# A two-layer decoder trunk on one core: first weight reads held behind a small write, output projections with three seven-product pairs and two added pairs, and new orders of the pieces in every kind of unit

## The chip, the cores and the metric

The kernel runs on one core of one Trainium2 chip; the other cores are idle. The metric is the device time of one execution in microseconds. The kernel before took 2147.89 us (median of three runs, 2144.24 to 2151.99). Lower is better.

## The reference

Two layers over x (256 tokens, 2048 features, float32). Each layer normalises x, projects it with w_in to gated linear attention (GLA) and stick-breaking attention heads, maps the heads' outputs with w_o, adds that to x, and adds a squared-ReLU MLP with 8192 hidden features. Cut to what the change touches:

```python
def hybrid_layer(x, attn_norm, w_in, ..., w_o, mlp_norm, w_up, w_down):
    h = rms_norm(x, attn_norm)
    proj = jnp.einsum('bsd,de->bse', h, w_in)
    ...
    mixed = jnp.concatenate([o_gla, o_sb], axis=-1)
    x = x + jnp.einsum('bse,ed->bsd', mixed, w_o)
    hm = rms_norm(x, mlp_norm)
    up = jnp.square(jax.nn.relu(jnp.einsum('bsd,df->bsf', hm, w_up)))
    return x + jnp.einsum('bsf,fd->bsd', up, w_down)
```

## The kernel before

**One product.** Every float32 weight and operand is split into a high part (rounded to the type float32r) and a low part (what is left). One product of a 128x128 block of the operand with a 128x512 piece of weights is three matmuls into one PSUM bank: high by high, high by low, low by high (L1198 to L1200; L613 to L615 in the older stages). The names in the profile are whi and wlo for a weight's parts: ACT copies raw to whi (L1066, the *cast*), DVE subtracts it from raw to get wlo (L1070, the *subtraction*). Four wlo buffers and five whi buffers (LOWS, RING) let both run ahead of PE.

**Units and steps.** From the first projection on, the work consists of *units* of 256 tokens by 1024 columns, with a depth of 2048 in 8 *pairs* of 128 rows. The kinds are g (the second GLA gate, 8 plain steps), o (output projection, two halves o0 and o1), up and down (MLP, four quarters of 8192, each with two up and two down units), and iv, ik, iq (a projection of the next layer, or of layer 0 at the start). A unit accumulates into eight PSUM banks; each pair's share of two token blocks by two column blocks is computed in one of three ways:
- *slow* pair: 8 products in two steps of four, 24 matmuls. Two casts and two subtractions of 128x1024.
- *fast* (seven-product) pair: the seven products of a Strassen scheme in four steps of 6, 6, 6 and 3 matmuls. DVE forms sums of the weights (L858: ts<-raw of 128x1024, raw<-ts,raw and raw<-raw of 128x512) and four subtractions, three of 128x1024 and one of 128x512. The operand needs sums too (forms, L439: four small DVE operations, L454 to L457, a copy on ACT, L471, and a subtraction on DVE, L475).
- *added* pair: 8 products in two steps of 12 matmuls, without DVE. POOL issues a DMA that reads the weights from HBM and rounds them on the way into a tile chi (L1033). ACT writes its negative into a tile dlo (L1037, the *negation*). POOL issues a second DMA that reads the same weights and adds them to dlo (L1040, the *correction*), which leaves the low part. There are three chi buffers (CAST) and two dlo buffers (ADDS).

**What sets the order.** In a unit, a list of pair numbers sets the order of the steps on PE (EACH, FEWER, MORE, OWN, L24 to L28; the two tuples behind a list name the fast and the added pairs). unit_order (L865) picks the list. A planner (Plan.run, L81) then lays all pieces of a phase out, with assumed lengths and due times, and so fixes the order of instructions on ACT and DVE; PE, SP and POOL keep the order in which the pieces were made. Each engine then runs its queue in that order, and waits in it. There are three phases: one before layer 0's attention (l = -1: iv, ik, iq of layer 0), and one behind the attention of each layer (l = 0: g, o, MLP, then iv, ik, iq of layer 1; l = 1: g, o, MLP).

**The opening.** Before the phase l = -1, SP loads x in four blocks, a vector of norm gains (t, 16 KB) and the first weights. PE turns x with the identity matrix ident, which POOL builds; it also turns the gains to a column (L334, copied by DVE in L335) which ACT needs for each operand cast (L500). 13 transposes of ident (L563) fill PE's time while it waits. Then 96 matmuls of a first value projection follow (L613 to L615) into acc_145; x blocks 1 to 3 are turned in between.

## Time and profile before

| | us |
|---|---|
| median of three runs | 2147.89 |
| the profiled execution | 2145.96 |
| its span, first to last instruction | 2144.3 |
| PE busy | 2124.8 |
| DVE busy | 1944.5 |
| ACT busy | 1403.3 |
| POOL busy | 234.5 |

The granted TensorE clock of the execution was 0.997 on average. PE's instructions are pipelined, so that "busy" says little of how fast it works: it has to be read by the distance of two starts in the timeline. Stages by first matmul, from the span's start: opening 13.9 to 42.2, iv/ik/iq of layer 0 to 163, attention of layer 0 to 299.5, gate unit and output projections to 370, MLP to 1090, iv/ik/iq of layer 1 to 1196, attention to 1359, gate unit and output projections to 1430, MLP to the end.

### The profile page before, as it was taken

To read this page: it belongs to the slowest core of one execution; us is meant where nothing else is said; L and a number is where in the kernel's file an instruction comes from. 1 tells how busy PE (TensorE), PEld (TensorE's weight loads), DVE (VectorE), ACT (ScalarE), POOL (GpSimd) and SP (SyncE) were. 2 spreads that over 40 slices of the span, in tenths; PEclk is the share of its full clock that TensorE was granted. 3 is DMA by queue.
4 is the path that set the end of the run, shared out by engine and by line. 5 is a ranking of instruction groups with operands and counts; after the bars stand their busy time and mean duration, and the time that the engine had idled before them with its cause. 6 is when DMAs were issued, how large, how long until landed. Compare 5 with 4: busy or idle time off the path is not lost.

```text
span 2144.3 us, 28255 instructions
## 1 busy us (share of the span) xinstructions
PE 2124.8 (99%) x10076; PEld 1765.1 (82%) x10076; DVE 1944.5 (91%) x2636; ACT 1403.3 (65%) x1853; POOL 234.5 (11%) x362
## 2 busy tenths in 40 slices
PE   8999999999999999999999999999999999999999
PEld 6788888888888888888888988888888888888887
DVE  5988878999999999999999796699999999999998
ACT  6666666676577566667766575666765765765764
POOL 0110000011111111111111100000111111111110
PEclk9999999999999999999999999999999999999999
DMA  7885365588888988988888644756888888888886
GB/s 247 245 236 179 118 187 196 167 246 252 258 251 246 268 239 253 266 245 238 252 258 251 191 138 137 224 162 204 260 241 258 254 258 247 246 255 256 248 244 196
DMA packets 146992, 488.74 MB, mean 228 GB/s; under 512 B 10298, under 2 KB 19074, under 8 KB 146852
## 3 DMA queue, kind: packets, MB, share of 16 engines
q1 hardware_dynamic: 103076, 327.55, 44.7%
q0 software_dynamic: 43776, 159.40, 31.6%
q8 instruction: 79, 1.29, 0.2%
q14 instruction: 61, 0.50, 0.1%
HBM read 484.81 MB, written 2.10 MB: 227 GB/s over the span
## 4 chain that ended last, share of the span: by engine, by line
PE 55%; issue 36%; POOL 5%; DMA 2%; DVE 1%; ACT 1%; POOLq 0%
POOL dlo L1040 3%; PE acc L613 3%; PE acc L615 2%; PE acc L614 2%; POOL chi L1033 2%; DMA dlo<-in_w_up_dram 1%; DMA dlo<-in_w_in_dram 1%; DMA dlo<-in_w_down_dram 1%; PE ps L1780 0%; DVE wlo L596 0%; DMA chi<-in_w_in_dram 0%; PE ps L724 0%; PE ps L1730 0%; PE ps L1773 0%; PE ps L778 0%
## 5 line engine op out<-in xcount | busy, mean ns | idle before, releaser
L1066 ACT ACTIVATE whi<-raw 128x1024 fp32r<-128x1024 f32 (+1 forms) x701 | 653.2, 955 | 364.6 <-DVE raw L858 209.9
L1070 DVE TENSOR_TENSOR wlo<-raw,whi 128x1024 fp32r<-128x1024 f32 (+1 forms) x701 | 760.9, 1091 | 70.0 <-ACT whi L1066 21.7
L1037 ACT ACTIVATE dlo<-chi 128x1024 fp32r<-128x1024 f32 x152 | 159.9, 1053 | 83.0 <-DMA chi<-in_w_in_dram 13.9
L1066 ACT ACTIVATE whi<-ts 128x1024 fp32r<-128x1024 f32 x165 | 174.4, 1057 | 53.5 <-DVE ts L858 29.2
L858 DVE TENSOR_TENSOR ts<-raw 128x1024 f32<-128x1024 f32 x165 | 200.7, 1216 | 3.9 <-DMA raw<-in_w_down_dram 2.2
L1070 DVE TENSOR_TENSOR wlo<-ts,whi 128x1024 fp32r<-128x1024 f32 x165 | 200.8, 1217 | 0.4 <-PE m__631_2940 L1199 0.2
L613 PE MATMUL acc<-whi,act 128*128 128x512 f32 (+2 forms) x384 | 142.1, 370 | 2.6 <-ACT whi L594 2.6
L615 PE MATMUL acc<-whi,act 128*128 128x512 f32 (+2 forms) x384 | 137.6, 358 | 0.0
L614 PE MATMUL acc<-wlo,act 128*128 128x512 f32 (+2 forms) x384 | 137.4, 358 | 0.0
L594 ACT ACTIVATE whi<-raw 128x1024 fp32r<-128x1024 f32 (+2 forms) x98 | 88.1, 906 | 64.7 <-PE acc L615 64.3
L596 DVE TENSOR_TENSOR wlo<-raw,whi 128x1024 fp32r<-128x1024 f32 (+2 forms) x98 | 100.4, 1030 | 30.4 <-ACT whi L594 29.5
L1033 POOL DMA_DIRECT2D chi<-in_w_up_dram x64 | 35.4, 555 | 759.2 <-PE m__2836_13416 L1200 142.1
L858 DVE TENSOR_TENSOR raw<-raw 128x512 f32<-128x512 f32 x165 | 112.8, 684 | 1.3
L858 DVE TENSOR_TENSOR raw<-ts,raw 128x512 f32<-128x512 f32 x165 | 112.5, 682 | 0.1
L1033 POOL DMA_DIRECT2D chi<-in_w_down_dram x64 | 35.4, 554 | 524.2 <-PE m__3624_17092 L1200 33.1
L1292 ACT ACTIVATE act<-act,st 128x512 f32<-128x512 f32 x88 | 60.5, 715 | 46.5 <-DVE act L858 46.4
L613 PEld LDWEIGHTS acc<-whi,act 128*128 128x128 f32 x384 | 72.9, 190 | 15.3 <-issue 3.4
L615 PEld LDWEIGHTS acc<-whi,act 128*128 128x128 f32 x384 | 72.9, 190 | 10.6
L614 PEld LDWEIGHTS acc<-wlo,act 128*128 128x128 f32 x384 | 73.0, 190 | 9.3 <-DVE wlo L596 0.4
L1040 POOL DMA_DIRECT2D dlo<-in_w_down_dram x64 | 54.7, 854 | 68.4 <-ACT dlo L1037 66.0
L475 DVE TENSOR_TENSOR act<-t,act 128x512 fp32r<-128x512 f32 x90 | 61.1, 682 | 0.0
L1040 POOL DMA_DIRECT2D dlo<-in_w_up_dram x64 | 54.8, 856 | 56.7 <-ACT dlo L1037 55.4
(4156 smaller groups left out, 5738.9 us busy)
## 6 DMA issues: line engine op xcount, KB each, us to landing
raw<-in_w_up_dram SPq DMA_DIRECT2D x96, 1024.0 KB, 7.8
raw<-in_w_down_dram SPq DMA_DIRECT2D x96, 1024.0 KB, 10.0
raw<-in_w_in_dram SPq DMA_DIRECT2D x72, 1024.0 KB, 5.3
chi<-in_w_up_dram POOLq DMA_DIRECT2D x64, 512.0 KB, 5.6
dlo<-in_w_up_dram POOLq DMA_DIRECT2D x64, 512.0 KB, 8.5
raw<-in_w_o_dram SPq DMA_DIRECT2D x32, 1024.0 KB, 5.2
chi<-in_w_down_dram POOLq DMA_DIRECT2D x64, 512.0 KB, 5.9
dlo<-in_w_down_dram POOLq DMA_DIRECT2D x64, 512.0 KB, 10.0
```

Source lines behind the costliest of these rows:

```text
L475: nc.vector.tensor_tensor(d[:, :, 1, :], src, f32(d[:, :, 0, :]), ALU.subtract)
L594: newest["hi"] = nc.scalar.activation(h, r, AF.Copy).ins
L596: newest["lo"] = nc.vector.tensor_tensor(lo[:, q : q + step, :width], r, f32(h), ALU.subtract).ins
L613: nc.tensor.matmul(o, xh[:, sl], whi[:, j, :width], start=first, stop=False)
L614: nc.tensor.matmul(o, xh[:, sl], wlo[:, j, :width], start=False, stop=False)
L615: st["mm"] = nc.tensor.matmul(o, xl[:, sl], whi[:, j, :width], start=False, stop=last).ins
L858: nc.vector.tensor_tensor(dst, a, b, op)
L1033: nc.gpsimd.dma_start(flat("h"), src)
L1037: nc.scalar.activation(box["l"], f32(box["h"]), AF.Copy, scale=-1.0)
L1040: nc.gpsimd.dma_start(flat("l"), src, accum_op=ALU.add)
L1066: nc.scalar.activation(box["h"][:, :n], src(), AF.Copy)
L1070: nc.vector.tensor_tensor(box["l"][:, :n], src(), f32(box["h"][:, :n]), ALU.subtract)
```

## The change

1. *Held first reads.* In the phase l = -1 each of the first three chi tiles gets a write of one column by ACT (held_tile), which reads ident. The DMA into the tile waits for that write. All three reads are now issued before the first correction.
2. *Output projections.* A unit o had two fast pairs (0, 1) and six slow ones. It now has three fast (0, 1, 2), two added (5 and 7 in o0, 5 and 6 in o1) and three slow pairs. Pair 2's operand sums are formed as those of 0 and 1 were.
3. *New orders* of the steps for every kind of unit except g, with a list LATER of its own for iv, ik, iq of layer 1. Which pairs are fast and added stays as it was there. In EACH the added steps move from places 6, 11, 16, 21 of 24 (counted from 0) to 3, 9, 16, 19.
4. The planner's assumed lengths change by some per cent, and it counts a chi read of a unit as possible only after the first product of the unit before (started); both act through the planned order alone.

Code that stays unused: SEEDED and SPARE are empty, so seeded_tail is not called, no tile of forms is placed otherwise, and product issues the same three matmuls.

```diff
-EACH = [0, 0, 1, 1, 1, 1, 2, 3, 3, 3, 3, 2, 5, 5, 5, 5, 4, 6, 6, 6, 6, 4, 7, 7], FAST, (2, 4)
+EACH = [7, 7, 5, 2, 5, 5, 1, 1, 5, 4, 1, 1, 3, 3, 3, 3, 4, 6, 6, 2, 6, 6, 0, 0], FAST, (2, 4)
...
+O0 = [4, 4, 7, 7, 6, 6, 1, 1, 1, 0, 1, 0, 5, 0, 0, 2, 2, 2, 2, 3, 5, 3], (0, 1, 2), (5, 7)
+O1 = [4, 5, 4, 0, 0, 0, 5, 0, 1, 1, 2, 1, 2, 6, 1, 2, 6, 2, 7, 7, 3, 3], (0, 1, 2), (5, 6)
+SEEDED = ()
+SPARE = ()
...
-OWN = {("up", 0): MORE, ("up", 0, 0): EACH}
...
+    ("up", 0): ([4, 0, 0, 0, 0, 5, 5, 4, 5, 5, 1, 1, 1, 3, 2, 1, 3, 3, 3, 6, 6, 6, 2, 6, 7, 7], (0, 1, 3, 5, 6), (2, 4)),
...
+    ("down", 1): ([0, 0, 3, 3, 3, 2, 3, 1, 1, 1, 1, 4, 5, 5, 5, 6, 5, 4, 6, 6, 6, 2, 7, 7], FAST, (2, 4)),
...
-        MM, TR, V2, V1, A2, A1 = 0.227, 0.108, 1.15, 0.61, 1.0, 0.55
+        MM, TR, V2, V1, A2, A1 = 0.2268, 0.109, 1.15, 0.62, 1.06, 0.60
...
             if kind == "o":
-                pairs = ((4, 5, 6, 7, 0, 1, 2, 3), (4, 5, 6, 0, 7, 1, 2, 3))[n2]
-                return [j for j in pairs for _ in range(4 if j < 2 else 2)], (0, 1), ()
+                return (O0, O1)[n2]
...
+            def held_tile():
+                box["h"] = tmp("chi", [P, 2, 512], F32R, bufs=CAST)
+                nc.scalar.activation(box["h"][:, 0, :1], ident[:, :1], AF.Copy)
...
-            h = add("POOL", 1.0, high, chi[-CAST] if len(chi) >= CAST else [], lag=LAND)
+            first = None
+            if l < 0 and len(chi) < CAST:
+                first = add("ACT", 0.2, held_tile, before[0])
+            h = add(
+                "POOL", 1.0, high, first, chi[-CAST] if len(chi) >= CAST else [],
+                started[u - 1] if u else [], lag=LAND,
+            )
...
-            if e < 2:
+            if e in O0[1] + O1[1]:
                 b = add("ACT", A1, scaled, p, take=1)
...
+                    started.setdefault(u, p[m])
```

How instructions stand at three places follows; rows give the line, the operation and out<-in with buffer numbers. Lines of the changed kernel are other ones: L1052 is the chi read, L1059 the correction, L1056 the negation, L1091 the cast, L917 the copy of a finished projection (L903 before).

First place: POOL at the program's start, before:

```order
masks.py:197 MEMSET ident 128x128
L1033 DMA chi_398<-in_w_in_dram 128x1024
masks.py:199 ISA
masks.py:199 AFFINE_SELECT ident<-ident 128x128
L1033 DMA chi_400<-in_w_in_dram 128x1024
L1040 DMA dlo_406<-in_w_in_dram 128x1024
L1033 DMA chi_413<-in_w_in_dram 128x1024
L1040 DMA dlo_408<-in_w_in_dram 128x1024
```

and now:

```order
masks.py:197 MEMSET ident 128x128
masks.py:199 ISA
masks.py:199 AFFINE_SELECT ident<-ident 128x128
L1052 DMA chi_398<-in_w_in_dram 128x1024
L1052 DMA chi_402<-in_w_in_dram 128x1024
L1052 DMA chi_405<-in_w_in_dram 128x1024
L1059 DMA dlo_418<-in_w_in_dram 128x1024
L1059 DMA dlo_451<-in_w_in_dram 128x1024
```

The first chi read stood ahead of the building of ident, and a correction followed the second read. Now ident comes first, and three reads stand together. On ACT three writes of 128x1 (L1047) stand at the start in place of two negations.

Second place: ACT where the opening ends and the first projection (iv) begins; acc_145 is the opening's result, raw_396 the weights of the first pair of iv. Before:

```order
L547 ACTIVATE t_54_368,ssq_95<-xb_94 128x512
L1066 ACTIVATE whi_72_411<-raw_396 128x1024
L903 ACTIVATE act_382<-acc_145 128x512
L1066 ACTIVATE whi_422<-raw_396 128x1024
L903 ACTIVATE act_382<-acc_145 128x512
L471 ACTIVATE act_440<-t_74_415 128x4x128
L1066 ACTIVATE whi_450<-raw_402 128x1024
L1066 ACTIVATE whi_460<-ts_442 128x1024
```

and now:

```order
L560 ACTIVATE t_54_368,ssq_95<-xb_94 128x512
L1091 ACTIVATE whi_71_410<-raw_396 128x1024
L917 ACTIVATE act_382<-acc_145 128x512
L1056 ACTIVATE dlo_418<-chi_398 128x1024
L917 ACTIVATE act_382<-acc_145 128x512
L1091 ACTIVATE whi_437<-raw_396 128x1024
L1056 ACTIVATE dlo_451<-chi_402 128x1024
L484 ACTIVATE act_461<-t_85_439 128x4x128
L1091 ACTIVATE whi_474<-raw_400 128x1024
```

The two negations that stood at the program's start are now here, one between the two copies of acc_145 and one behind the second cast. On PE the first two steps of iv use the two casts of raw_396, the third uses raw_400, and the fourth is the added step with chi_398 and dlo_418.

Third place: ACT where the gate unit of layer 0 begins; acc_2595 (now acc_2598) is the last result of the attention stage, raw_2902 (now raw_2905) the gate unit's first weights. Before:

```order
L403 ACTIVATE st_2836<-st_2836 128x4
L1037 ACTIVATE dlo_2912<-chi_2904 128x1024
L1037 ACTIVATE dlo_2914<-chi_2906 128x1024
L1066 ACTIVATE whi_619_2917<-raw_2902 128x1024
L903 ACTIVATE act_2881<-acc_2595,st_393 128x512
L1066 ACTIVATE whi_2925<-raw_2902 128x1024
L903 ACTIVATE act_2881<-acc_2595,st_393 128x512
L1066 ACTIVATE whi_2943<-raw_2908 128x1024
```

and now:

```order
L816 ACTIVATE act_2700<-ps_2822 128x512
L1091 ACTIVATE whi_615_2911<-raw_2905 128x1024
L694 ACTIVATE t_585_2835<-act_2700 128x512
L412 ACTIVATE st_2839<-st_2838 128x4
L413 ACTIVATE st_2839<-st_2839 128x4
L917 ACTIVATE act_2884<-acc_2598,st_393 128x512
L1091 ACTIVATE whi_2916<-raw_2905 128x1024
L917 ACTIVATE act_2884<-acc_2598,st_393 128x512
L1091 ACTIVATE whi_2934<-raw_2907 128x1024
```

Two negations stood ahead of the unit's first cast. Now the cast stands ahead of the last head's norm (L694, L412, L413), and the unit's two negations follow behind its sixth and seventh cast. Layer 1 has the same orders at this place.

More of the change, by code (lines that the diff above doesn't have):

```diff
@@ L870, in unit_order @@
             if kind == "o":
-                pairs = ((4, 5, 6, 7, 0, 1, 2, 3), (4, 5, 6, 0, 7, 1, 2, 3))[n2]
-                return [j for j in pairs for _ in range(4 if j < 2 else 2)], (0, 1), ()
+                return (O0, O1)[n2]
             if u and units[u - 1][0] == "down" and kind == "iv":
                 return FEWER
+            if l >= 0 and kind in AHEAD:
+                return LATER
             return OWN.get((kind, n2, q), OWN.get((kind, n2), EACH))
@@ L1086, in ordered @@
         sums13 = []
-        chi, late, made_halves = [], [], {}
+        chi, late, made_halves, started = [], [], {}, {}
         every = [
@@ L1108, in added_steps @@
             kind, q, _ = units[u]
[L1109 removed]
+            op = {"o": mixed, "up": hm, "down": up.get(q)}.get(kind, hT)
             def blk(k, tt):
@@ L1188, in steps, with product @@
             ]
-        def product(m, blocks, box, begin, end):
-            if begin:
+        def product(m, blocks, box, begin, end, seeded):
+            if begin and m not in seeded:
                 banks[m] = bank(m)
@@ L1197, in product @@
                 o = banks[m]
-                nc.tensor.matmul(o, ah, h, start=begin and i == 0, stop=False)
-                nc.tensor.matmul(o, ah, lo, start=False, stop=False)
-                nc.tensor.matmul(o, al, h, start=False, stop=end and i + 1 == len(blocks))
+                check = dict(skip_group_check=True) if m in seeded else {}
+                nc.tensor.matmul(
+                    o, ah, h, start=begin and i == 0 and m not in seeded, stop=False, **check
+                )
+                nc.tensor.matmul(o, ah, lo, start=False, stop=False, **check)
+                nc.tensor.matmul(
+                    o, al, h, start=False, stop=end and i + 1 == len(blocks), **check
+                )
         def bk(m):
```

74 lines of the change are left out of this document (66 added, 8 removed).

## The prediction

> **What bounds the kernel now.** I read the page's first part, then the waits of PE, then the timeline at the places those waits name.
>
> ```profile
> PE 2124.8 (99%) x10076; PEld 1765.1 (82%) x10076; DVE 1944.5 (91%) x2636; ACT 1403.3 (65%) x1853; POOL 234.5 (11%) x362
> ```
>
> PE is never idle for long, so only three things can shorten the run: fewer matmuls, matmuls at full rate, and the few waits. The timeline of PE shows what a matmul costs, here at the dearest wait for a correction (columns: start, duration, instruction, idle before it).
>
> ```profile
> 2046.68 0.39 PE L1200 MATMUL m__3836_18106<-whi,act 128*128 128x512 f32 x1
> 2046.91 0.39 PE L1198 MATMUL m__3833_18093<-chi,act 128*128 128x512 f32 x1
> 2048.51 0.50 PE L1199 MATMUL m__3833_18093<-dlo,act 128*128 128x512 f32 x1 [1.22 <-DMA dlo<-in_w_up_dram]
> 2048.85 0.39 PE L1200 MATMUL m__3833_18093<-chi,act 128*128 128x512 f32 x1
> ```
>
> Matmuls start 0.227 us apart (2046.68 to 2046.91), whatever their 0.39 us duration says: they are pipelined. A wait costs more than its idle time: 2046.91 to 2048.51 is 1.60, so 1.37 is lost where 1.22 is called idle, and the next start is 0.34 later, 0.11 too many. So a wait costs its idle time plus 0.27. The waits of PE (total, times, longest), shortened to the rows that carry a term:
>
> ```profile
> PE m__3833_18093 L1199 <- DMA dlo<-in_w_up_dram: 1.2, 1, 1.2
> PE m__156_800 L1199 <- DMA dlo<-in_w_in_dram: 0.9, 1, 0.9
> ...
> PE m__626_2935 L1199 <- DVE wlo L1070: 0.8, 1, 0.8
> PE m__2637_12424 L1199 <- DVE wlo L1070: 0.8, 1, 0.8
> PE m__80_434 L1199 <- DVE wlo L1070: 0.6, 3, 0.2
> ...
> PE m__1063_5046 L1199 <- DMA dlo<-in_w_down_dram: 0.2, 1, 0.2
> ```
>
> Seven rows of that view name a correction tile (dlo); from the 1.2 to the 0.2 they add up to 3.8 us. With 0.27 each, late corrections cost 5.7 us. Four windows (length, then busy time of PE, PEld, DVE, ACT, POOL, then granted clock) give the stages: the opening from its first matmul, the first projection after it, the gate unit and output projections of layer 0, the MLP of layer 0.
>
> ```profile
> 13.91:42.20 28.29, 27.48 (x121) 22.20 (x121) 18.85 (x30) 20.62 (x46) 0.00 (x0) 0.90 0.89 289
> 42.20:85.58 43.38, 42.80 (x181) 33.24 (x180) 40.53 (x60) 28.70 (x36) 5.68 (x8) 1.00 0.80 226
> 299.50:370.00 70.50, 69.74 (x320) 57.72 (x319) 62.15 (x80) 49.70 (x69) 0.20 (x1) 1.00 0.66 205
> 370.00:1090.00 720.00, 718.58 (x3259) 595.46 (x3258) 693.29 (x899) 481.57 (x610) 90.08 (x128) 1.00 0.83 246
> ```
>
> The base of the sum is the profiled execution: 2145.96 us, of which 2144.3 is the span. The median of the three runs, 2147.89, is 1.9 higher.
>
> **The opening.** All engines in one timeline; the last row is the wait for the third block of x.
>
> ```profile
> 0.82 1.28 ACT L257 ACT_TABLE_LOAD   x1 [0.82 <-PEq L1818]
> 1.36 0.69 POOL L1033 DMA_DIRECT2D chi<-in_w_in_dram  x1 [0.33 <-issue]
> 1.83 0.46 SPq L325 DMA_DIRECT2D t<-in_attn_norm_dram  x1
> 8.27 1.06 ACT L1037 ACTIVATE dlo<-chi 128x1024 fp32r<-128x1024 f32 x1 [6.16 <-DMA chi<-in_w_in_dram]
> 8.47 0.24 PE L334 MATMUL ps<-ident,t 32*128 32x32 f32 x1 [2.41 <-DMA t<-in_attn_norm_dram]
> 8.75 0.19 DVE L335 COPY gcol_a<-ps 128x32 f32<-128x32 f32 x1 [8.75 <-PE ps L334]
> 9.63 0.89 POOL L1040 DMA_DIRECT2D dlo<-in_w_in_dram  x1 [6.66 <-ACT dlo L1037]
> 10.83 1.06 ACT L1037 ACTIVATE dlo<-chi 128x1024 fp32r<-128x1024 f32 x1 [1.51 <-DMA chi<-in_w_in_dram]
> 11.79 1.55 ACT L500 ACTIVATE act<-ps,gcol_a 128x256 fp32r<-128x256 f32 x4
> 13.22 2.20 ACT L594 ACTIVATE whi<-raw 128x512 fp32r<-128x512 f32 x4
> 13.91 0.79 PE L613 MATMUL acc<-whi,act 128*128 128x512 f32 x1 [2.63 <-ACT whi L594]
> 19.07 0.53 PE L615 MATMUL acc<-whi,act 128*128 128x512 f32 x1
> 24.01 1.09 PE L490 MATMUL ps<-ident,xb 128*128 128x128 f32 x8 [0.81 <-DMA xb<-in_x_dram]
> ```
>
> The gain column is ready at 8.75 + 0.19 = 8.94, yet ACT starts the four operand casts at 11.79: it stood in the second negation, which waited for its chi read until 10.83. The change moves both negations behind the opening. ACT then starts at about 9.0, its first weight cast follows 1.43 later (11.79 to 13.22) and the first matmul 0.69 after that: 11.1 instead of 13.9, 2.8 us. The gain vector itself took 6.6 us to land, beside the chi reads. In the changed kernel these go out after ident and the table load (0.82 + 1.28 = 2.1), near 2.3 instead of 1.36, but three in a row. I take half a microsecond from that: 3.3.
> The 28.29 us window has a granted clock of 0.90, so 2.8 us of it are half-rate time, all before 19.07. A first matmul at about 10.6 closes the pause between the warm-up transposes and it; of 0 to 2.8 I take 1.0. The window of the Trainium skill's "TensorE: Matmul & The Clock Gate", Part 1 (full rate after one busy window of about 3.4 us, windows running freely) agrees with a recovery at 19 after a restart at 13.9; by it the gain here would be an estimated 0 to 2.4, by chance of the window's phase.
> The 0.81 wait at 24.01 stands behind correction reads (9.63 and one more) which now come after the opening: 0.7. Opening: -5.0, ends -1 and -8.
>
> **The start of the first projection.** Here the moved negations return: ACT's queue (the second place of the orders) has one negation ahead of the second copy of the opening's result and of the second weight cast, and one right behind it.
>
> ```profile
> 42.40 0.60 ACT L903 ACTIVATE act<-acc 128x512 f32<-128x512 f32 x1 [3.59 <-PE acc L615]
> 42.89 1.05 ACT L1066 ACTIVATE whi<-raw 128x1024 fp32r<-128x1024 f32 x1
> 43.84 0.59 ACT L903 ACTIVATE act<-acc 128x512 f32<-128x512 f32 x1
> 43.98 1.23 DVE L1070 TENSOR_TENSOR wlo<-raw,whi 128x1024 fp32r<-128x1024 f32 x1 [2.78 <-ACT whi L1066]
> DMA to landing us min/median/max: 7.2/9.3/12.2
> ```
>
> On the clock of these rows: copy 42.40, negation 42.89 to 43.84, copy to 44.32, cast to 45.38, its subtraction to 46.6. PE wants it after one slow step of 12 and one matmul, 42.20 + 2.95 = 45.15: 1.5 lost. The correction is issued after the negation, at 44.2, and lands 7.2 to 12.2 later (last row: the dlo reads from 42 to 163 us); I take 8.0, so 52.2. PE wants it after 30 matmuls and the wait, at 50.5: 1.7 lost. That makes 3.2 for what is 0.26 today. Today's 43.38 us window is that projection, 180 matmuls of 0.227 or 40.9 us, so it loses 2.5 in all, mostly DVE being late for weights (the m__80 row); those 3.2 us give DVE time, so I let 2.3 of them go. +0.6, ends -0.5 and +4.
>
> **Output projections.** A fast pair takes 21 matmuls where a slow one takes 24: one more in each of four units, 12 x 0.227 = -2.7. On DVE a slow pair needs two full-width operations, a fast one four and three half-width ones, an added pair none: 2 x 5.5 + 6 x 2 = 23 before, 3 x 5.5 + 3 x 2 = 22.5 after. Pair 2's operand forms add six small DVE operations a layer, each under the 1.23 us of a full-width one, so under 7.4: they lie in the 8.35 us that DVE has free in the 70.50 us window, and would cost that much if it had none.
>
> **The start of the gate unit.** This is an edit that the words on the change don't announce.
>
> ```profile
> 296.53 1.99 ACT L1037 ACTIVATE dlo<-chi 128x1024 fp32r<-128x1024 f32 x2
> 299.50 1.23 DVE L1070 TENSOR_TENSOR wlo<-raw,whi 128x1024 fp32r<-128x1024 f32 x1 [1.56 <-ACT whi L1066]
> 299.52 0.50 PE L1198 MATMUL m__626_2935<-whi,act 128*128 128x512 f32 x1
> 300.78 0.50 PE L1199 MATMUL m__626_2935<-wlo,act 128*128 128x512 f32 x1 [0.76 <-DVE wlo L1070]
> ```
>
> Two negations stand ahead of the unit's first weight cast; the subtraction is done only at 300.7, and PE loses 1.03 + 0.11 = 1.14, in each layer. The new ACT order (the third place of the orders) has that cast ahead, and the negations behind the sixth and seventh cast, some 11 us into the unit. Next late is the second subtraction (done 302.54 now, as its copy waits for PE), wanted at 299.52 + 2.95 = 302.47: 0.07. -2.2 in both layers, ends 0 and -2.3. The corrections then leave about 13 and 15 us into the unit and, with 10 us to land, are there at 25; PE wants them after 120 matmuls, at 27 and 30.
>
> **Corrections.** The rows that price them: an issue from the timeline of POOL, and the page's medians from issue to landing.
>
> ```profile
> 2036.04 0.86 POOL L1040 DMA_DIRECT2D dlo<-in_w_up_dram  x1 [0.35 <-ACT dlo L1037]
> dlo<-in_w_up_dram POOLq DMA_DIRECT2D x64, 512.0 KB, 8.5
> dlo<-in_w_down_dram POOLq DMA_DIRECT2D x64, 512.0 KB, 10.0
> ```
>
> There are two dlo buffers, so a correction waits for the added step two uses back, then for negation and issue (1.06 + 0.35 = 1.4 us). Today's list leaves an added step (2.72) and two fast pairs (4.77 each) in between, 12.3 us, in 74 of 152 uses: with the chi matmul ahead of it 12.3 + 0.2 - 1.4 = 11.1 us for the landing. Seven landings took longer, the longest from 2036.04 to 2048.5, 12.5 us. Counted on the new lists, 21 of 168 uses have 12.3 and 6 have 11.6 (the added step that opens the first up unit of a later quarter: behind the last step of pair 4 in the down unit ahead come 15 matmuls of pair 6, 12 of pair 2 and 24 of pair 7, 51 x 0.227); the rest have 12.9 to 30. At today's rate the 21 cost 5.7 x 21/74 = 1.6; the 6, with 10.4 us for a landing whose median is 8.5, I put at 0.2 each. 2.8 instead of 5.7: -2.9, ends -5.5 and +3.
>
> **New orders elsewhere.** In the MLP DVE is busy 96% (693.29 of 720); its work stays, its place in a unit moves. No wait of that stage names DVE now. For waits that I can't see I add +1.0, ends 0 and +12.
>
> **Sum.** -5.0 + 0.6 - 2.7 - 2.2 - 2.9 + 1.0 = -11.2: 2134.8 on the profiled execution; and as the median stands 1.9 above that execution, I go half of it up: 2135.7.
>
> **Rivals.**
> (1) The three reads still collide with the first transfers. For it: held by one microsecond only, and half a megabyte more; against: they no longer block ACT. The gain vector lands 1 later instead of earlier, so 1.8, clock and x gain nothing: 3.2 less than forecast, 2138.9. The Trainium skill's "DMA: Bandwidth & Descriptors", Queues, rings and completion order, speaks for it: engines take the queues in turn, packet by packet, so a short transfer waits behind the other queue's packets; the 6.6 us landing fits.
> (2) Everything clears: the gain vector lands near 6, PE turns it 2.4 us earlier than at 8.47 and the first matmul is at 8.7 (-5.2), clock -1.8, x -0.8, no correction late (-5.7), no new wait: with +0.6, -2.7 and -2.2 that is -17.8, 2129.1. For it: no chi read is issued before 2.1; against: the vector's own landing of 6.6.
> (3) DVE comes late in the new lists: one wait like m__80's (0.2 + 0.27) in three of four of some 40 units is +14 in place of the +1.0: 2148.7, no change. Against: same DVE work, same four wlo buffers.
> (4) Slower: corrections land late at the tight uses, since output projections and the next unit's reads share the rings. A mean landing of 12.4 would cost the 21 uses 1.3 each and the 6 uses 2.0: 39 instead of 2.8, 2172. It decides from a mean of about 11.5, where 21 x 0.4 + 6 x 1.1 = 15 undo the whole gain. Against: medians of 8.5 and 10.0.
>
> **Chances.** Forecast 0.55 (its own range 2132 to 2139), (1) 0.20, (2) 0.12, (3) 0.08, (4) 0.05. A measurement tells about 0.3% from no change, here 2141.4. Faster: 0.55 + 0.12 + 0.13 of (1) = 0.80; same 0.07 + 0.08 = 0.15; slower 0.05. The range 2129 to 2142.5 leaves out (3), (4) and some of (2).
>
> **What would show it.** First matmul near 10.6, the operand casts of ACT directly behind the gain column; the end of the opening near 37; two waits at the next unit's start, for a subtraction and for dlo; no wait at the gate units' first matmuls; 12 matmuls fewer; dlo waits of about 2 us idle in all. A first matmul after 12, or a row of DVE waits inside the MLP, proves me wrong.

## The result and the profile after

| | before | changed |
|---|---|---|
| median, beside each other | 2146.4 (4 runs, 2144.24 to 2151.99) | 2134.8 (4 runs, 2134.17 to 2136.6) |
| profiled execution / its span | 2145.96 / 2144.3 | 2136.6 / 2134.9 |
| mean granted clock | 0.997 | 0.999 |

The ratio of the times is 0.9941 (95% interval 0.9924 to 0.9957): 12 us faster, 9 to 16. The forecast was 2135.7 with a range of 2129.0 to 2142.5. The same kernel once more, beside the last experiments: 2136.3 (6 runs, 2134.92 to 2137.93), ratio 0.9953 (0.9936 to 0.997).

The first part of the page and the waits of PE (total us, times, longest), changed kernel:

```profile
PE 2119.2 (99%) x10064; PEld 1762.4 (83%) x10064; DVE 1945.3 (91%) x2650; ACT 1414.4 (66%) x1868; POOL 265.7 (12%) x394
```

```profile
PE ps L503 <- DMA xb<-in_x_dram: 2.9, 2, 2.4
PE acc L626 <- ACT whi L607: 2.5, 1, 2.5
PE ps L576 <- POOL ident masks.py:199: 1.4, 1, 1.4
PE m__904_4303 L1227 <- DMA dlo<-in_w_up_dram: 1.1, 1, 1.1
PE ps L737 <- DVE act L700: 1.1, 2, 0.5
PE m__82_434 L1227 <- DVE wlo L1095: 0.8, 1, 0.8
PE m__229_1148 L1224 <- DVE act L871: 0.6, 1, 0.6
PE m__82_434 L1224 <- ACT whi L1091: 0.3, 1, 0.3
```

Twelve matmuls fewer (10064 for 10076), one dlo row where seven stood, and no row of a gate unit's first matmuls (m__626, m__2637) any more; the 2.41 us wait for the gain vector is gone too. The wait for x blocks at the top has grown from 0.8 to 2.9. The first projection's start (m__82, where m__80 stood) now waits for a cast and for a subtraction, and m__229 is new: the third projection's first use of a PSUM bank, which DVE has not emptied.

Where the 9.4 us between the spans come from, taken from the starts of PE's products at the borders of the stages:

| stage | before | after | difference | forecast |
|---|---|---|---|---|
| up to the first projection | 42.20 | 39.51 | -2.69 | -5.0 |
| three projections of layer 0 | 43.39 + 42.03 + 40.57 | 43.69 + 40.80 + 41.55 | +0.05 | +0.6 (start) |
| two gate units | 23.86 + 23.86 | 22.99 + 23.05 | -1.68 | -2.2 |
| four output projections | 2 x 87.03 | 2 x 85.91 | -2.24 | -2.7 |
| the rest of both MLP phases | 796.19 + 669.77 | 795.87 + 667.39 | -2.70 | -2.9 + 1.0 |
| attention and end | | | -0.16 | 0 |

The opening of the changed kernel in the timeline, and the start of the first projection behind it:

```profile
2.63 1.78 POOL L1052 DMA_DIRECT2D chi<-in_w_in_dram  x3 [1.24 <-ACT chi L1047]
6.05 0.19 DVE L345 COPY gcol_a<-ps 128x32 f32<-128x32 f32 x1 [6.05 <-PE ps L344]
6.28 1.57 ACT L513 ACTIVATE act<-ps,gcol_a 128x256 fp32r<-128x256 f32 x4 [3.78 <-DVE gcol_a L345]
9.44 0.63 ACT L607 ACTIVATE whi<-raw 128x512 fp32r<-128x512 f32 x1 [1.59 <-DMA raw<-in_w_in_dram]
10.12 0.51 PE L626 MATMUL acc<-whi,act 128*128 128x512 f32 x1 [2.53 <-ACT whi L607]
14.56 0.63 ACT L607 ACTIVATE whi<-raw 128x512 fp32r<-128x512 f32 x1 [1.33 <-DMA raw<-in_w_in_dram]
16.09 1.97 PE L503 MATMUL ps<-ident,xb 128*128 128x128 f32 x8 [2.45 <-DMA xb<-in_x_dram]
...
40.21 1.05 ACT L1056 ACTIVATE dlo<-chi 128x1024 fp32r<-128x1024 f32 x1
41.63 1.06 ACT L1091 ACTIVATE whi<-raw 128x1024 fp32r<-128x1024 f32 x1
42.74 0.49 PE L1224 MATMUL m__82_434<-whi,act 128*128 128x512 f32 x1 [0.35 <-ACT whi L1091]
44.00 0.50 PE L1227 MATMUL m__82_434<-wlo,act 128*128 128x512 f32 x1 [0.76 <-DVE wlo L1095]
```

ACT now does the operand casts at 6.28, right behind the gain column, and the first matmul starts at 10.12 instead of 13.91. But the four quarters of the first weights arrive one by one (a cast at 9.44, the last at 14.56, each behind a DMA), and PE stands 2.45 us before the second block of x. The three chi reads, 1.5 MB, issued from 2.63 on, are in flight beside both. The windows show what follows (length, busy time of PE, PEld, DVE, ACT, POOL, granted clock, DMA share, GB/s):

```profile
10.12:16.09 5.97, 3.30 (x12) 2.10 (x13) 3.44 (x6) 2.62 (x5) 0.00 (x0) 1.00 1.07 401
16.09:19.50 3.41, 3.41 (x12) 3.09 (x13) 1.38 (x4) 2.24 (x5) 0.00 (x0) 0.50 1.05 388
...
10.12:39.51 29.39, 26.72 (x120) 21.86 (x121) 18.95 (x33) 21.02 (x46) 0.00 (x0) 0.94 0.84 302
...
319.81:405.72 85.91, 85.91 (x391) 71.12 (x390) 81.09 (x114) 60.92 (x87) 11.16 (x16) 1.00 0.85 249
```

The first matmuls run at full clock, and the wait is followed by 3.41 us at half clock. From the first matmul to the end the opening takes 29.39, where it took 28.29: 3.79 were won ahead of the first matmul and 1.10 lost behind it. The last row is the output projections of layer 0, in which the record shows PE busy throughout.

### The profile page after: what moved, and what is told of

It is laid out like the page before. It is cut to its first block, busy times and chain, and to the rows that moved or that the text cites. A ratio compares the mean times of both kernels' runs of the same rounds, so it can differ in the third digit from the quotient of the medians.

```text
span 2134.9 us, 28247 instructions
## 1 busy us (share of the span) xinstructions
PE 2119.2 (99%) x10064; PEld 1762.4 (83%) x10064; DVE 1945.3 (91%) x2650; ACT 1414.4 (66%) x1868; POOL 265.7 (12%) x394
## 4 chain that ended last, share of the span: by engine, by line
PE 66%; issue 26%; POOL 4%; DVE 2%; DMA 2%; ACT 1%; SPq 0%; POOLq 0%; ACTq 0%; DVEq 0%
PE acc L626 3%; PE acc L628 3%; PE acc L627 3%; POOL dlo L1059 2%; POOL chi L1052 2%; DMA xb<-in_x_dram 1%; DVE wlo L1095 1%; DMA raw<-in_w_in_dram 1%; DMA dlo<-in_w_up_dram 0%; PE ps L1869 0%; DVE wlo L609 0%; PE ps L737 0%; PE ps L1819 0%; PE ps L1862 0%; PE ps L791 0%
## 5 line engine op out<-in xcount | busy, mean ns | idle before, releaser
L1095 DVE TENSOR_TENSOR wlo<-raw,whi 128x1024 fp32r<-128x1024 f32 (+1 forms) x689 | 745.1, 1088 | 44.8 <-ACT whi L1091 31.3
L1091 ACT ACTIVATE whi<-raw 128x1024 fp32r<-128x1024 f32 (+1 forms) x689 | 640.8, 950 | 210.3 <-DVE raw L871 94.5
L1056 ACT ACTIVATE dlo<-chi 128x1024 fp32r<-128x1024 f32 x168 | 177.2, 1055 | 121.9 <-DMA chi<-in_w_down_dram 19.3
L1091 ACT ACTIVATE whi<-ts 128x1024 fp32r<-128x1024 f32 x169 | 179.1, 1060 | 109.8 <-DVE ts L871 82.6
L871 DVE TENSOR_TENSOR ts<-raw 128x1024 f32<-128x1024 f32 x169 | 205.9, 1218 | 3.8 <-DMA raw<-in_w_o_dram 2.5
L1095 DVE TENSOR_TENSOR wlo<-ts,whi 128x1024 fp32r<-128x1024 f32 x169 | 205.9, 1219 | 0.8 <-PE m__2113_9932 L1227 0.5
L1052 POOL DMA_DIRECT2D chi<-in_w_up_dram x64 | 38.0, 593 | 559.2 <-PE m__831_3958 L1228 40.2
L1052 POOL DMA_DIRECT2D chi<-in_w_down_dram x64 | 35.6, 556 | 513.8 <-PE m__1619_7630 L1228 34.8
L1059 POOL DMA_DIRECT2D dlo<-in_w_up_dram x64 | 58.0, 906 | 46.2 <-ACT dlo L1056 41.2
L1059 POOL DMA_DIRECT2D dlo<-in_w_down_dram x64 | 54.0, 843 | 57.3 <-ACT dlo L1056 51.7
```

The source lines that it names most:

```text
L871: nc.vector.tensor_tensor(dst, a, b, op)
L1052: nc.gpsimd.dma_start(flat("h"), src)
L1056: nc.scalar.activation(box["l"], f32(box["h"]), AF.Copy, scale=-1.0)
L1059: nc.gpsimd.dma_start(flat("l"), src, accum_op=ALU.add)
L1091: nc.scalar.activation(box["h"][:, :n], src(), AF.Copy)
L1095: nc.vector.tensor_tensor(box["l"][:, :n], src(), f32(box["h"][:, :n]), ALU.subtract)
```

## Experiments

Each kernel was timed beside the kernel before; the ratios are to that. Two sums from the traces serve as a yardstick beside the time: the end of the opening, and *late corrections*, by which is meant what goes beyond 0.227 us between two starts of PE ahead of a product with a dlo tile, added up over the execution without those under 0.12 us (4.96 in the profiled execution of before; the forecast's 5.7 was worked out from the idle time in another way).

### One part undone

**No held writes.**

```diff
-            if l < 0 and len(chi) < CAST:
-                first = add("ACT", 0.2, held_tile, before[0])
```

> The changed kernel without the held writes: the first three chi reads are issued as early as in the kernel before, and the first two negations return to the front of ACT. Theory A (the held writes shorten the opening by 2.7, and cost 1.6 at the start of the first projection, where the negations stand instead): the first matmul of the opening is near 13.9 again, the two waits for a second weight cast and its subtraction at the first projection's start go, and the time is 2.7 - 1.6 = 1.1 above the changed kernel's 2134.8, near 2135.9. Rival B (the opening got shorter for another reason than the hold, by when the gain vector happened to land): first matmul near 10.1, 1.6 less, near 2133.2. Rival C (the hold gave the whole 5.0 that was forecast, and the 2.45 us wait for the second x block is not its work): near 2138.2.

2137.27 (5 runs, 2136.5 to 2138.2), ratio 0.9957 (0.9945 to 0.997). The timeline of its opening, and the windows of opening and first projection:

```profile
6.91 1.06 ACT L1056 ACTIVATE dlo<-chi 128x1024 fp32r<-128x1024 f32 x1 [4.80 <-DMA chi<-in_w_in_dram]
10.76 1.06 ACT L1056 ACTIVATE dlo<-chi 128x1024 fp32r<-128x1024 f32 x1 [2.80 <-DMA chi<-in_w_in_dram]
13.85 0.79 PE L626 MATMUL acc<-whi,act 128*128 128x512 f32 x1 [5.46 <-ACT whi L607]
```

```profile
13.85:42.02 28.17, 26.61 (x120) 21.54 (x121) 18.79 (x33) 20.74 (x46) 0.00 (x0) 0.94 0.90 300
42.02:84.29 42.27, 42.09 (x181) 33.40 (x180) 39.71 (x56) 28.37 (x35) 5.64 (x8) 1.00 0.79 224
```

ACT is blocked until 11.8 again, although the gain column was ready at 6.8 here: the block is what the held writes remove, not the late gain vector. The opening ends at 42.02 (+2.5), and the first projection takes 42.27 instead of 43.69 (-1.4). That is theory A: over half of the hold's gain of 2.5 is given back by the negations, which in the changed kernel stand between the copies of the opening's result.

**The old lists of the output projections.**

```diff
-                return (O0, O1)[n2]
+                pairs = ((4, 5, 6, 7, 0, 1, 2, 3), (4, 5, 6, 0, 7, 1, 2, 3))[n2]
+                return [j for j in pairs for _ in range(4 if j < 2 else 2)], (0, 1), ()
...
-            if e in O0[1] + O1[1]:
+            if e < 2:
```

> The changed kernel with the lists of the output projections of before (two seven-product pairs, none added), all else kept. Theory A (these lists are worth their count of matmuls): 12 matmuls more, 12 x 0.227 = 2.7 more than 2134.8, near 2137.5, with the gate unit starting as in the changed kernel. Rival B (the added pairs also bring waits of their own, for banks and corrections in and behind these units, that go with them): 1 to 2 more only, near 2136. Rival C (the third seven-product pair also relieves DVE, which comes late without it): 4 or more, 2139 and above, with new DVE waits in the two units.

2135.87 (5 runs, 2135.72 to 2137.91), ratio 0.9952 (0.994 to 0.9965). The time does not tell this from the changed kernel (2134.8 and 2136.3). The window of one layer's output projections does:

```profile
318.81:405.84 87.03, 87.03 (x398) 72.31 (x397) 80.10 (x106) 57.25 (x80) 1.73 (x2) 1.00 0.66 205
```

87.03 against 85.91, to the hundredth the same in layer 1: 1.12 a layer for six matmuls, where the count says 1.36. The other 0.24 is a small wait that the new lists bring, here in the changed kernel (PE, its weight load, and ACT):

```profile
337.79 0.68 ACT L1489 ACTIVATE t<-m__685_3269,gcol_b 128x512 f32<-128x512 f32 x1
338.16 0.40 PE L1228 MATMUL m__625_2930<-whi,sx 128*128 128x512 f32 x1
338.52 0.19 PEld L1224 LDWEIGHTS m__691_3296<-whi,act 128*128 128x128 f32 x1 [0.40 <-ACT t L1489]
338.86 0.40 PE L1227 MATMUL m__691_3296<-wlo,act 128*128 128x512 f32 x1
```

The product m__691 starts when ACT has read a finished result (m__685) out of its bank, and two starts of PE are 0.36 and 0.34 apart instead of 0.227. Layer 1 has the same pair at 1395.79 and 1396.13; the kernel with the old lists has neither. So the lists are worth 2.24, and a little of rival B is true. The gate unit kept its 23.01.

**The old lists of steps.** EACH, FEWER, MORE and OWN of the kernel before; the first of them:

```diff
-EACH = [7, 7, 5, 2, 5, 5, 1, 1, 5, 4, 1, 1, 3, 3, 3, 3, 4, 6, 6, 2, 6, 6, 0, 0], FAST, (2, 4)
+EACH = [0, 0, 1, 1, 1, 1, 2, 3, 3, 3, 3, 2, 5, 5, 5, 5, 4, 6, 6, 6, 6, 4, 7, 7], FAST, (2, 4)
...
+LATER = EACH
```

> The changed kernel with the lists of steps of before in the up, down and projection units, all else kept (held reads, output projections, planner). Theory A (the lists decide the time that a correction has to land): seven or so late corrections return, dlo waits of 3 to 4 us idle or 5 to 6 with their restart against 1.8 in the changed kernel, so +3.9; the first projection's first correction is wanted later in that list, so its start loses 1.5 less: near 2134.8 + 3.9 - 1.5 = 2137.2. Rival B (the planner's rule on when a chi read may start decides it, not the lists): dlo waits stay near 1.8, and the time is 2133.3 to 2134.8. Rival C (the new lists cost DVE waits elsewhere, 1.8 by the trace, that go too): 2135.4.

2135.5 (5 runs, 2133.06 to 2138.44), ratio 0.9947 (0.9933 to 0.9961): undoing the lists cost nothing that can be measured, and the runs spread over 5.4 us. In the profiled execution, the slowest of the five, late corrections are 3.03 against 1.55 and the first projection takes 44.46. The waits:

```profile
PE m__1690_7966 L1222 <- DMA dlo<-in_w_down_dram: 1.3, 1, 1.3
PE m__76_428 L1222 <- DVE wlo L1090: 1.1, 1, 1.1
```

Late corrections return, but fewer than seven. Against the changed kernel's profile this execution loses 0.77 in the first projection, 0.64 in the second, 0.36 in the first projection of layer 1 and 0.57 in the two MLPs, and wins 0.75 in the third projection. The time alone leaves theory A and rival C open.

**No rule on the start of chi reads.**

```diff
-                started[u - 1] if u else [], lag=LAND,
+                lag=LAND,
```

> The changed kernel without the rule that a chi read follows the first product of the unit before its own. Theory A (this rule, not the lists, moved the two negations behind the gate unit's first weight casts): they stand ahead of the first cast again, PE waits some 0.8 us there in each layer, 1.03 + 0.11 with the restart against 0.4 to 0.5 now, so +0.7 in each of two layers: near 2136.2, with the rest the same. Rival B (in the MLP the rule also delays reads, so without it the corrections land with more margin): the 1.8 us of dlo waits go as well, near 2134.4. Rival C (the rule spreads the reads, and without it corrections collide): dlo waits of 4 us and more, 2139.

2136.31 (5 runs, 2135.96 to 2138.7), ratio 0.9955 (0.9942 to 0.9967). The timeline at the gate unit of layer 0:

```profile
292.50 1.99 ACT L1056 ACTIVATE dlo<-chi 128x1024 fp32r<-128x1024 f32 x2
294.39 1.04 ACT L1091 ACTIVATE whi<-raw 128x1024 fp32r<-128x1024 f32 x1
...
296.75 0.50 PE L1227 MATMUL m__626_2938<-wlo,act 128*128 128x512 f32 x1 [0.76 <-DVE wlo L1095]
```

The negations stand ahead of the first cast again, the 0.76 wait is back, and the gate units take 23.84 and 23.82. Theory A: this one rule moved them.

### One part alone, on the kernel before

**Held writes alone.** held_tile as in the change, and its piece:

```diff
+            first = None
+            if l < 0 and len(chi) < CAST:
+                first = add("ACT", 0.2, held_tile, before[0])
```

> The kernel before with the held writes alone added. Theory A (the hold is worth what the changed kernel shows, an opening that ends at 38.3 to 39.7 instead of 42.0 to 42.2, about 3): first matmul 10 to 10.7, opening end near 39.3; in the old list the first correction is wanted only after two slow steps and a fast one, so nothing is lost at the first projection's start: 2145.9 - 2.9 = 2143.0. Rival B (the hold works only together with the new orders, since the negations' place is the planner's): first matmul near 13.9, 2145.9. Rival C (the negations, now inside the first projection, cost there what they gave, 1.5): 2144.5.

2147.29 (12 runs, 2143.78 to 2154.02) against 2147.53, ratio 1.0 (0.999 to 1.0011). The first matmul came at 10.29 (not rival B), the opening ended at 38.51, 3.7 earlier, and the three projections took 127.69, 1.7 more: the cost that rival C names, and that theory A took for nothing. That leaves 2.0, the end of what the interval allows. Where did it go in this execution? The waits name dlo:

```profile
PE m__893_4271 L1207 <- DMA dlo<-in_w_up_dram: 2.9, 1, 2.9
...
PE m__3385_15985 L1207 <- DMA dlo<-in_w_down_dram: 1.3, 1, 1.3
PE m__3076_14540 L1207 <- DMA dlo<-in_w_down_dram: 1.1, 1, 1.1
PE m__156_803 L1207 <- DMA dlo<-in_w_in_dram: 1.1, 1, 1.1
PE m__3694_17430 L1207 <- DMA dlo<-in_w_down_dram: 1.1, 1, 1.1
```

Late corrections are 9.53 here, 4.96 in the profiled execution of before, although the whole orders of PE and DVE are the same in both kernels, and those of ACT and POOL differ at the first reads, negations and held writes alone. So this difference of several us is put down to the execution; no kernel with the old lists was profiled twice. The longest of these waits cost more than itself (rows of PE, then the window behind the wait):

```profile
489.20 0.80 PE L1207 MATMUL m__893_4271<-dlo,act 128*128 128x512 f32 x1 [2.86 <-DMA dlo<-in_w_up_dram]
490.22 0.63 PE L1206 MATMUL m__896_4283<-chi,act 128*128 128x512 f32 x1
490.65 0.63 PE L1207 MATMUL m__896_4283<-dlo,act 128*128 128x512 f32 x1
488.90:492.31 3.41, 3.11 (x7) 2.48 (x8) 1.55 (x2) 0.00 (x0) 0.00 (x0) 0.50 1.04 297
```

A stretch of 3.41 us at half clock follows it in the middle of the MLP, with starts 0.43 apart: the seven spacings from 489.20 to 492.34 lose another 1.5 us, of which 0.4 is counted in the 9.53. The opening's gain is shown by the stage, not by the time.

**The rule alone.**

```diff
+                started[u - 1] if u else [], lag=LAND,
...
+                    started.setdefault(u, p[m])
```

> The kernel before with the rule alone that a chi read follows the first product of the unit before its own. Theory A (the rule does nothing but move the two negations of each layer behind the gate unit's first weight casts): the subtraction waits of 0.76 at the gate units' first matmuls go, 2.3 for both, late corrections stay at the old lists' 3 to 9.5: near 2147.5 - 2.0 = 2145.5. Rival B (the rule also spaces the reads, so that corrections land sooner): late corrections below 2, 2142. Rival C (the second subtraction takes the wait over): 2147.5.

2146.3 (12 runs, 2141.14 to 2148.74) against 2146.38, ratio 0.9994 (0.9984 to 1.0005). The gate units take 23.01 and 23.05 (before 23.86 twice), 1.66 less, as theory A has it; late corrections 2.33 in the profiled execution, which was the fastest of the twelve. The second subtraction takes 0.3 of it for itself (rival C in part): in layer 0 three starts of PE, around the product that wants it, are 300.56, 301.00 and 301.33, where 0.227 between two would be the rate.

**The lists of steps alone.** EACH, FEWER, LATER and OWN of the change, with the line that picks LATER:

```diff
+            if l >= 0 and kind in AHEAD:
+                return LATER
```

> The kernel before with the new lists of steps of the up, down and projection units alone (no held writes, old output projections, no rule on chi reads, old planner constants). Late corrections (time beyond 0.227 us ahead of a product with a correction tile) so far: 4.96, 9.53 and 3.03 us in the three profiled executions with the old lists, 0 to 1.70, 0.8 in the mean, in the seven with the new ones. Theory A (the lists decide it, and the executions of one list scatter): late corrections below 2, against 5.0 to 9.5, less 1 to 1.5 of new DVE waits: 2147.5 - 4 = near 2143.5. Rival B (the old lists' profiled executions were unlucky draws; undoing the lists in the changed kernel cost 0.7 by the medians): near 2146.5. Rival C (the lists work only with the other parts): late corrections of 4 or more, 2147.5.

2139.37 (12 runs, 2137.36 to 2143.32) against 2146.38, ratio 0.9965 (0.9956 to 0.9975): 7.5 us faster, 5.4 to 9.4, the largest effect of any part alone and more than theory A's 4. The profiled execution was the slowest of the twelve (its opening ended at 45.02). By its stages the projections win 2.39 against before (iv 42.23, ik 40.80, iq 40.57) and the MLPs 0.89 and 2.16. The window of the first projection:

```profile
45.02:87.25 42.23, 42.05 (x181) 33.39 (x180) 39.70 (x56) 28.37 (x35) 5.63 (x8) 1.00 0.79 223
```

Late corrections in all profiled executions:

```
old lists:  4.96 (before)  9.53 (held writes alone)  3.03 (old lists in the changed kernel)  2.33 (rule alone)
new lists:  1.55 and 0.21 (changed, twice)  0.00  0.47  1.04  2.06  and in the kernels below  1.70  0.12  0.41  0.83
```

On average 5.0 against 0.8. The margins of all uses tell the lists apart more sharply. From the fifteenth use on, a landing came less than 1 us ahead of its product in 24 of 138 uses before, and in 8 of 154 in the changed kernel. In all fourteen profiles it is 22 to 29 uses with the old lists and 8 to 11 with the new ones; with the lists alone it is 8 of 138. So the lists decide how many corrections run tight, and how much is late.

What stays open is why undoing them in the changed kernel cost nothing by the time. Its corrections are as tight as before (26 of 154). Its negations do start sooner behind the last product that reads their tile: a median of 0.10 us over all uses, 0.27 before. But the rule alone has 0.12 and the lists alone 0.04, both with the old planner constants. So the new constants, which were not run alone, are not shown to be the reason.

### Held longer

The opening of the changed kernel suggests that the reads were not held long enough. Here POOL writes the column, from a block of x, so that the reads leave when that block has landed:

```diff
-            def held_tile():
+            def high(held=l < 0 and len(chi) < CAST):
                 box["h"] = tmp("chi", [P, 2, 512], F32R, bufs=CAST)
-                nc.scalar.activation(box["h"][:, 0, :1], ident[:, :1], AF.Copy)
...
+                if held:
+                    nc.gpsimd.tensor_copy(box["h"][:, 0, :1], xb[1][:, 0, :1])
                 nc.gpsimd.dma_start(flat("h"), src)
...
-                first = add("ACT", 0.2, held_tile, before[0])
+                first = before[0]
```

> The changed kernel with the three first tiles written by POOL from the second block of x instead of by ACT from the identity, so that the three chi reads go out only when that block has landed. Theory A (the three reads, 1.5 MB, are what makes the first weight casts wait for their raw quarters and PE wait 2.45 us for the second x block): the chi reads leave near 12, that wait and the half-rate window behind it go, and the opening ends near 36.5 instead of 39.5: near 2134.8 - 2.7 = 2132.1. Rival B (SP's own reads fill the queue, the chi reads do not matter): the wait stays, 2134.8. Rival C (the reads then collide with the third and fourth x block): a wait of 1 to 2 at the next transposes, 2134.

2130.5 (5 runs, 2128.9 to 2132.03), ratio 0.992 (0.9907 to 0.9932). Timeline and windows:

```profile
8.18 2.21 ACT L607 ACTIVATE whi<-raw 128x512 fp32r<-128x512 f32 x4
...
10.69 1.49 POOL L1048 CAST chi<-xb 128x1 fp32r<-128x1 f32 x3 [9.30 <-DMA xb<-in_x_dram]
12.12 1.78 POOL L1049 DMA_DIRECT2D chi<-in_w_in_dram  x3
12.37 1.03 PE L503 MATMUL ps<-ident,xb 128*128 128x128 f32 x8
```

```profile
9.09:34.38 25.29, 25.24 (x123) 20.73 (x121) 18.48 (x33) 21.25 (x47) 4.11 (x7) 1.00 1.00 361
34.38:76.64 42.26, 42.17 (x182) 33.32 (x180) 39.70 (x56) 29.17 (x36) 6.51 (x9) 1.00 0.92 249
```

Theory A, and more than it forecast: the four casts run back to back from 8.18 to 10.39 with no DMA wait, the second block is there by 10.69 instead of 16.09, no part of the opening is at half clock, and it ends at 34.38. The first projection loses nothing to the negations either, as the first of them now stands ahead of the copies. So by the stages 5.1 of the gain over the changed kernel is the opening, and 1.4 is this new place of the negation.

**Held until the fourth block.**

```diff
-                    nc.gpsimd.tensor_copy(box["h"][:, 0, :1], xb[1][:, 0, :1])
+                    nc.gpsimd.tensor_copy(box["h"][:, 0, :1], xb[3][:, 0, :1])
```

> As the kernel before this one, but the three first tiles are written from the fourth block of x, so the reads go out when all of x has landed. Theory A: no x block waits at all, the opening ends near 36.3, the reads still land before the first negation: near 2131.9, the same as with the second block or 0.2 less. Rival B (the reads are now late, and collide with the first reads of the projection's weights): PE waits at the first projection's start for a raw read or for the first correction, 1 to 4 us: 2133 to 2136. Rival C (POOL, which stands in the held write, also holds back something that the opening needs): an opening that ends after 39.

2129.31 (4 runs, 2128.06 to 2129.97), ratio 0.9914 (0.99 to 0.9928). The reads leave at 19.75, the opening ends at 33.91, the first projection takes 42.23. None of the rivals' waits came, and here too the first negation stands ahead of the copies.

**Held until the second block, negations ahead.** As the first of these, and the first two negations come ahead in the plan (early is true for the first two tiles):

```diff
+                with tc.issue_after(last_cast) if early else nullcontext():
                     nc.scalar.activation(box["l"], f32(box["h"]), AF.Copy, scale=-1.0)
...
-                started[u - 1] if u else [], lag=LAND,
+                started[u - 1] if u else [], lag=0.0 if early else LAND,
```

last_cast is the opening's last weight cast on ACT; the negations then stand behind the last sum of squares.

> As the hold on the second x block, and besides the first two negations stand on ACT directly behind the opening's last sum of squares, ahead of the copies of the opening's result. Theory A (the negations between the copies and ahead of the second weight cast cost the 0.51 + 1.03 + 0.11 us that PE waits at the first projection's start): those two waits shrink to the 0.1 to 0.5 that the copies alone make, so 1.2 less than with the hold on the second block alone: near 2130.9. Rival B (the second weight cast is late for the copies and the raw read anyway): the waits stay, 2132.1. Rival C (two negations there make the first weight cast late): a wait at the projection's first matmul of 0.5 to 1.5, 2132.5.

2129.84 (5 runs, 2129.47 to 2133.16), ratio 0.992 (0.9907 to 0.9933). The first projection takes 42.25, the same as without: the second block alone had already cured that. The third projection is 0.7 to 0.9 shorter (41.27 for 41.95 and 42.21), since its wait for a bank shrinks.

**Both.** Fourth block and negations ahead, the two diffs above together; and the changed kernel once more beside it, without an edit.

> The changed kernel with both that were faster: the three reads held until the fourth x block has landed, and the first two negations ahead of the copies of the opening's result. Theory A (the two are independent): the opening ends near 34 as with the fourth block, and the first projection takes 124.3 instead of 125.2 to 126.0: 2129.3 - 0.9 = near 2128.4. Rival B (reads issued near 20 land after 33, the negations wait for them and hold up the first weight cast): a wait of 0.5 to 3 at the projection's first matmul, 2129 to 2132.

> The changed kernel itself once more, beside the others on one chip. If the scatter of late corrections between executions is what theory A says: 0 to 2 us of late corrections, an opening that ends between 38.3 and 39.7, and a time of 2134 to 2137; the kernel with the fourth block and the early negations is then 6 to 7 faster. Rival: an opening or corrections outside these, which would mean that the chip, not the kernel, sets them.

2129.69 (6 runs, 2127.11 to 2130.08), ratio 0.9918 (0.9903 to 0.9934), and 2136.32 for the changed kernel. In the profile with both, the opening ends at 33.38 and the three projections take 124.3, as theory A has it, but the 0.9 that this should bring does not show in the time: the four kernels that hold longer are not told apart from each other; all are 4 to 7 us below the changed kernel, and beat both kernels. In the changed kernel's second profile the opening ends at 39.39, with the same wait (2.46 us at 15.97); late corrections are 0.21.

## Why the prediction was right

The time was right to 1 us (2134.8 for 2135.7), and the mechanisms of most terms held. That it was so close is in part luck. In the pair of profiles, for which the sum was made, the spans differ by 9.4 where the sum says 11.2: the opening came 2.3 short, the output projections and gate units 1.0 together, and the first projection, the corrections and the new waits made up for 1.5. The medians differ by 11.6, but the kernel before scatters over 10 us.

- **Opening, -5.0: measured -2.7.** Its first step held: ACT is freed, the operand casts stand behind the gain column, and the first matmul came at 10.1 for "about 10.6", 3.8 won for 3.3. The 1.0 for the clock came out too, by other means. Before, the half-clock stretch from the first matmul on was 5.4 us (13.91 to 19.35) and lost 2.7 (the prediction calls its 2.8 the length); now the first matmuls are at full clock, and a new stretch of 3.41 us behind the x block loses 1.7. The step that failed is "the 0.81 wait at 24.01 stands behind correction reads ... which now come after the opening: 0.7": PE's idle time from the first matmul on grew from 0.81 to 2.67. The corrections do come later, but the chi reads that they follow are still in the opening: two had gone out at 1.36 and 2.38 and the third at 10.19, now all three leave from 2.63 on, ahead of the second x block, and its wait is 2.45. This is rival (1) in a place that it did not name: not the gain vector but the weight quarters and x are late. Holding the reads longer gave the rest, an opening that ends at 34, beyond the 37 of the forecast.
- **First projection, +0.6: +0.30 in that unit.** Two parts: the new list alone takes 1.16 off (42.23), the held negations put 1.4 on (42.27 without them, 43.69 with). At the start, the waits for the second cast and its subtraction cost 1.65, for the 1.5 of the forecast; the forecast wait of 1.7 for dlo did not come, as that correction landed 6.1 us after its issue where 8.0 was taken. The unit's other losses fell from over 2 to 1.2, not to 0.2. Two misses nearly cancel here, which is luck.
- **Output projections, -2.7: -2.24.** Twelve matmuls, 1.36 a layer, less 0.24 for the wait for a bank that ACT empties, a term that the forecast did not have. DVE's added operations were hidden: no DVE row of PE's waits belongs to these units.
- **Gate units, -2.2: -1.68.** The mechanism was right, and undone by the one rule it comes from. The size was off by the second subtraction, 0.31 a layer where 0.07 was taken.
- **Corrections -2.9, new waits +1.0.** In the pair of profiles late corrections fell by 3.4; the one in the second projection (1.10 of that unit's -1.23) was one of the seven rows. What is left of the 9.4 behind all these terms is +0.3, for the new waits less what the lists won elsewhere; one new wait, of 0.98, came at the third projection's first bank. So by this pair the two terms are right to 1.2. By the medians the size is open: the lists alone brought 7.0 (5.4 by the stages of one execution), and undoing them cost 0.7 at most. The forecast priced 27 tight uses at the rate of one execution of before, and such a sum scatters: 2.3 to 9.5 in four executions with the old lists.
- **Other rivals.** No DVE row inside the MLP (3), no late corrections beyond 2.1 with the new lists (4). The first matmul of (2), near 8.7, was reached by the kernels that hold longer (8.3 to 9.1).

Built up from the kernel before, the parts nearly add: -7.0 for the lists by the medians, and by the stages -2.7 for the opening, +1.4 for the negations behind it, -2.2 and -1.7, which makes -12.2 for the measured -11.6. Alone, held writes (-0.2) and rule (-0.1) do not show in the time, with about 2 us of uncertainty each. Taken out of the changed kernel they do not add: any one part costs 0 to 2.5, and the lists, the largest, next to nothing. Stages of the trace, which repeat to some hundredths where no DMA is waited for, told the small parts apart; the times could not.

## What to carry to other kernels

A transfer that nothing needs soon should be held by what needs the queue before it, here a one-column write that reads the last tile of the urgent load; a hold of a microsecond only moved the collision to the next load, and the longer one was worth 4 to 7 us more. Such a write belongs on an engine with nothing behind it that is wanted, here POOL; a long hold on ACT was not run. And a wait that hangs on DMA landings must be priced as a distribution: several executions of before, and the margins of all uses, not the sum of those that happened to be late in one profile.

## What was not expected of the hardware

- The kernel before ran from 2141.29 to 2151.8 in 23 runs, the one with both edits of the last experiment from 2127.11 to 2130.08 in 6; late corrections were 2.33, 4.96 and 9.53 in profiles of three kernels with the same order on PE. That the scatter comes from late landings fits the fewer tight uses of the second kernel (9 for 24), but most of these executions have no trace that would show it.
- An idle PE of 2.45 us was followed by 3.41 us at a granted clock of 0.50; in the second profile 2.46 us of idle time by products 0.43 us apart from 16.82 to 20, and in the kernel with held writes alone 2.86 us by half clock from 488.90 on. In the 3.41 us ahead of the slow stretch PE was busy for 0.98, 0.94 and 0.86 us. A pause alone does not tell: the one of 2.53 us before the first matmul of the changed kernel (7.58 to 10.12) was followed by full clock; it lay across two such stretches, with 1.75 and 2.32 us of work. The Trainium skill's "TensorE: Matmul & The Clock Gate", Part 1, has the clock fall after one idle window of about 3.4 us; here shorter pauses were enough.
- With the chi reads behind x, the opening moved its data at 361 GB/s with the DMA engines busy throughout, against 302 GB/s and a share of 0.84.
